# Two transformer blocks on one core: modulation rows spread in program order, the context split off the end of a feed-forward, and the query products put last

## The chip, the cores and the metric

The kernel runs on one core of a Trainium2 chip. The metric is the device time of one launch, in microseconds. Of the kernel before, three runs gave 2831.24, 2831.26 and 2832.66 us; the median is 2831.26 us.

## The reference

The program is a hybrid layer followed by a conditioned block, on 512 tokens of width 1024, all in fp32.

The first block normalizes 16 meta tokens and the 512 tokens, projects them, runs retention, differential attention and a short convolution side by side, merges the three by gates, and ends with a feed-forward `x + relu(norm(x) @ w_up)^2 @ w_down` of width 4096 and a norm.

The second block takes that result as its latent tokens, and 256 context tokens beside them. Nine modulation vectors of width 1024 steer it:

```python
m  = split(silu(c)     @ w_ada + b_ada, 9)     # for the latent tokens
mc = split(silu(c_ctx) @ w_ada + b_ada, 9)     # for the context
x     = residual(x,     swiglu(modnorm(x,     g[0], m[0],  m[1]),  w1, w3, w2), g[1], m[2],  0.5)
h_ctx = residual(h_ctx, swiglu(modnorm(h_ctx, g[0], mc[0], mc[1]), w1, w3, w2), g[1], mc[2], 0.5)
q, k, v, gates = project(modnorm(x, g[2], m[3], m[4]), modnorm(h_ctx, g[2], mc[3], mc[4]))
```

The feed-forward is 2816 wide. Then follow neighbourhood attention and attention from low-rank query and key latents (768 and 256 wide), a gated merge and a second feed-forward, for the latent tokens only. All of `m` is needed, and the first five vectors of `mc`.

## The kernel before

Activations lie with the model width on the 128 partitions in 8 slabs and the tokens along the free axis. Each fp32 operand is split into a high and a low part, and each product is three matmuls (high x high, high x low, low x high). Weights come as units of 512 KB by DMA from the SP queue into `raw`, three buffers deep; ScalarE writes the high part `whi` (line 132), VectorE or GpSimd the low part `wlo` (line 136). `low_parts(V, G)` lets the two take turns, `low_parts(V, V)` gives all to VectorE. Results collect in PSUM, in four buffers that take turns (`DEEP`), and are read out ("evacuated") by VectorE and ScalarE.

The class `Emitter` writes the program out. Its items are products (`gemm`), calls and background work. It keeps a program clock: each matmul adds its columns / 2.4 + 3 ns (`tick`). A background generator is advanced by one step each time that the clock has gained its pace (`background(fn, pace)`); `drain` writes out all that is left of it; `after(ns, fn)` delays a piece of work by that much of the program clock. What is written out in this order is then ordered on each engine by the framework's scheduler, which goes by program order but lets an instruction that it takes to be ready go ahead of others on its engine.

The stages that matter here, in order:

- **The feed-forward of the first block** (`up_evac`, `down_evac`, from line 1084): four groups g of 8 up and 8 down units, each unit 24 matmuls of 512 columns. An up result takes two VectorE steps (`ut`, lines 1045 and 1046), the high part by ScalarE (`uh`) and the low part (`ul`).
- **The modulation rows** (`ada_bg`, line 975): the product with `w_ada` isn't done on TensorE. Its 72 row tiles of 128 x 1024 (`wa`, 512 KB each, three buffers, loaded by SP) are multiplied with the spread conditioning `sb` and summed by one VectorE instruction (line 995). Tiles 0 to 39 are taken twice, for the context (`wx`) and the latents. That makes 112 such instructions and the coefficients `cf` after them. All run in the background of groups 0 to 2 of the first feed-forward, one in 2250 ns of the program clock, and are drained before group 3.
- **Block 2's first feed-forward** (`ffn`, `XC`): 22 hidden tiles in three groups (6, 8, 8). For each, `pair` makes two units (`w1`, `w3`) over 258 context columns and 512 latent columns; two of the columns carry the shift. Then `products` multiplies the hidden tiles with `w2`.
- **Its end** (`f1_tail`): the products of the last group come as context and second half of the latents (512 columns), then the first half (256). Beside the latter runs `update` (line 1174) for the 512 columns that are ready: norm, residual, and the next modulated input, in 11 slots of VectorE, ScalarE and GpSimd work.
- **Projections** (`kv`, line 1388, and after): key and value latents over context and second half, beside the `update` of the first half; drain; key and value latents over the first half, with the same weights loaded again; six query units; then key, value, rotated-query and query products, whose results are written to DRAM for the attention.

Of the kernel before, what the change touches and what calls it, by code (L numbers as in the profile page):

```python
# [14 lines left out]
D = 1024  # L15
# [243 lines left out]
def emit(tc, d, out, dbg=None, stop=None):  # L259
# [10 lines left out]
    def act(o, i, f=AF.Copy, **kw):  # L270
        A.activation(o, i, f, **kw)
# [684 lines left out]
    def mod(k, s=0):  # L956
        return S["modc"][:, s, 8 * k:8 * k + 8]

    def open_f():
        for n in ("m2", "bina", "xhl"):  # L960
            pools.close(n)
        p = S["hlx"] = pools.open("hlx")
        S["XH"] = p.tile([128, KT, 514], F32R, name="XH")
        S["XL"] = p.tile([128, KT, 514], F32R, name="XL")
        S["modc"] = p.tile([128, 2, 72], F32, name="modc")
        S["cf"] = p.tile([128, 9, 8], F32, name="cf")
        S["R4"] = p.tile([128, 768], F32, name="R4")
# [3 lines left out]
        S["CL"] = p.tile([128, KT, 258], F32R, name="CL")  # L971
        S["up"] = pools.open("up")
        S["ad"] = pools.open("ad")

    def ada_bg():

        p = S["ad"]
        sb = p.tile([128, 2, D], F32, name="sb")
        SP.dma_start(sb, d["cc"].partition_broadcast(128))
        act(sb, sb, AF.Silu)  # L980
        W, todo = [], list(range(72))

        def load():
            if todo:
                w = p.tile([128, D], F32, name="wa", tag="wa", bufs=3)
                SP.dma_start(w, d["wa"][todo.pop(0)])
                W.append(w)
        for _ in range(3):
            load()
        yield  # L990
        for j in range(72):
            w = W.pop(0)
            for s_ in ((1, 0) if j < 40 else (0,)):
                o = w if s_ == 0 else p.tile([128, D], F32, name="wx", tag="wx")
                V.tensor_tensor_reduce(o, w, sb[:, s_, :], 1.0, 0.0, ALU.mult, ALU.add,  # L995
                                       S["modc"][:, s_, j:j + 1])
                if s_ == 0:
                    load()
                yield
        V.tensor_add(S["modc"][:, 0, :], S["modc"][:, 0, :], col("bada", 0, 72))  # L1000
        V.tensor_add(S["modc"][:, 1, 0:40], S["modc"][:, 1, 0:40], col("bada", 0, 40))

        def gcol(i):
            return col("g", 8 * i, 8)
        for o, i, m_, s_ in ((AF0, 0, 1, 0), (A0C, 0, 1, 1), (A2X, 2, 4, 0), (A2C, 2, 4, 1), (A4, 4, 7, 0)):
            V.tensor_scalar_add(cf(o), mod(m_, s_), 1.0)
            V.tensor_mul(cf(o), cf(o), gcol(i))
        V.tensor_mul(cf(AF0), cf(AF0), col("final", 0, 8))
        for o, i, m_, s_, w in ((B1X, 1, 2, 0, 0.5), (B1C, 1, 2, 1, 0.5), (B3, 3, 5, 0, None), (B5, 5, 8, 0, 0.5)):
            V.tensor_mul(cf(o), mod(m_, s_), gcol(i))  # L1010
            if w is not None:
                V.tensor_scalar_mul(cf(o), cf(o), w)
        yield

    def shift_cols(kx, kc):
        todo = [(S["XH"], S["XL"], 512 + i, mod(kx)) for i in range(2)]
        if kc is not None:
            todo += [(S["CH"], S["CL"], 0, mod(kx)), (S["CH"], S["CL"], 1, mod(kc, 1))]
        for h_, l_, o, m_ in todo:
            act(h_[:, :, o], m_)  # L1020
            sub_lo(V, l_[:, :, o], m_, h_[:, :, o])

    def ctx_ops():

        pools.close("ad")
        p = S["fp"]
# [57 lines left out]
    em.call(open_f)  # L1084
    em.background(ada_bg, 2250)
    for g in range(4):
# [32 lines left out]
    def ffn(tag, w1, w3, w2, mode, ntok, pool, Rk, down, head, tail):  # L1119
# [26 lines left out]
        for gi, (k0, nk) in enumerate(grp):  # L1146
# [27 lines left out]
    def update(c0, c1, p, b, a, bc=None, ac=None, spilled=False, late=1500):  # L1174


        xe = min(c1, 512)
        n = xe - c0
        Ry, acc = S["Ry"][:, c0:c1], S["accy"][:, c0:c1]
# [8 lines left out]
        def parts(k):  # L1188

            yield S["y"][:, k, c0:xe], S["x"][:, k, c0:xe], b, a, S["XH"][:, k, c0:xe], S["XL"][:, k, c0:xe], 0  # L1190
            if ctx:
                yield S["y"][:, k, xe:c1], CR[k], bc, ac, S["CH"][:, k, 2:258], S["CL"][:, k, 2:258], n

# [71 lines left out]

    MQ = 96.0 ** -0.5

    def open_pj():
# [8 lines left out]
        p = S["pj"] = pools.open("pj", side="right")  # L1277
        S["QH"] = p.tile([128, 6, 512], F32R, name="QH")
        S["QL"] = p.tile([128, 6, 512], F32R, name="QL")
        S["Rq"] = p.tile([128, 512], F32, name="Rq")  # L1280
        S["aq"] = p.tile([128, 512], F32, name="aq")
        S["tmpq"] = p.tile([128, 512], F32, name="tmpq")
        for n_, w in (("rotT", 128), ("ropeC", 512), ("ropeS", 512)):
# [3 lines left out]
    def open_kvp():  # L1287
        pools.close("hid")
        p = S["kvp"] = pools.open("kvp")
        S["KH"] = p.tile([128, 2, 768], F32R, name="KH")  # L1290
# [5 lines left out]
        S["krt"] = p.tile([32, 768], F32, name="krt")  # L1296
        S["krs"] = p.tile([32, 2, 768], F32R, name="krs")

    def lat_evac(j, hi, lo, acc, g, nt, last, done):
# [118 lines left out]
    def open_na():  # L1418
        em.flush_after()
        pools.close("pj")  # L1420
        pools.close("kvp")
        p = S["onap"] = pools.open("onap", side="right")
# [425 lines left out]

    def f2_tail(products):
        products([(256, 256)])  # L1850
# [125 lines left out]
```

## Time and profile before

| | us |
|---|---|
| median of three runs | 2831.26 |
| profiled execution | 2835.28 |
| its span, first to last instruction | 2833.3 |

The profile is of one execution. Its own time is 2835.28 us, 2.0 us more than the span; the steps are summed against that. PE is TensorE, PEld its weight load, DVE VectorE, ACT ScalarE, POOL GpSimd, and SP the engine whose queue issues the DMAs. PEclk is the granted clock of TensorE as a share of 2.4 GHz. A wait in the trace is put down to what released it.

### The profile page before, as it was taken

Reading aid. Unit: us, or ns where it says so; the run is one execution under the profiler, and the core shown is the slowest. Engines: PE = TensorE matmul, PEld = TensorE weight load, DVE = VectorE, ACT = ScalarE, POOL = GpSimd, SP = SyncE. Lnnn points to the kernel's source line nnn. Section 1 sums busy time; section 2 is a strip of 40 time slices with the busy share of each in tenths; the row PEclk is TensorE's granted clock in tenths of the full one; section 3 lists DMA queues with packets and bytes.
Section 4 is the critical chain, followed back from the end, with each engine's and each line's share of the span. In section 5 each row is a group of like instructions: output and inputs, shape, how many; then the busy total and the mean of one; then the engine's idle time right before and its main releaser. Section 6 shows DMA issues by size and latency. Waiting matters only on the chain.

```text
span 2833.3 us, 42915 instructions
## 1 busy us (share of the span) xinstructions
PE 2736.0 (97%) x16308; PEld 2405.3 (85%) x16308; DVE 1620.0 (57%) x3318; ACT 1092.5 (39%) x2201; POOL 849.9 (30%) x710
## 2 busy tenths in 40 slices
PE   9999999999999889899999999979999999899997
PEld 8889988888878667788888888868889998899897
DVE  6554422377757999555223233496576876834346
ACT  4333322445534222243222122354455665633233
POOL 0223323433324233242111112442333224323224
PEclk9999999999999999999999999989999999999998
DMA  4222222443225658332121221334643424332324
GB/s 136 73 68 91 96 97 93 129 125 102 83 93 191 205 195 295 114 108 68 53 75 60 61 66 60 93 117 156 179 102 103 133 62 162 133 97 90 93 94 127
DMA packets 115998, 316.95 MB, mean 112 GB/s; under 512 B 21680, under 2 KB 35376, under 8 KB 115536
## 3 DMA queue, kind: packets, MB, share of 16 engines
q1 hardware_dynamic: 115792, 314.21, 35.5%
q8 instruction: 129, 2.11, 0.3%
q14 instruction: 77, 0.63, 0.1%
HBM read 279.09 MB, written 13.83 MB: 103 GB/s over the span
## 4 chain that ended last, share of the span: by engine, by line
PE 80%; DVE 14%; issue 3%; ACT 2%; DMA 0%; POOL 0%; POOLq 0%; DVEq 0%; SPq 0%; ACTq 0%
PE psg L231 49%; PE pss L231 22%; DVE wlo L136 2%; DVE wa L995 2%; DVE wx L995 1%; PE pss L277 1%; PE pst L827 1%; PE pss L278 1%; PE pss L279 1%; PE pst L1731 1%; PE pst L1717 1%; PE pss L1528 1%; PE pst L824 0%; DVE ut L1045 0%; DVE mg L1224 0%
## 5 line engine op out<-in xcount | busy, mean ns | idle before, releaser
L136 POOL TENSOR_TENSOR wlo<-raw,whi 128x512 fp32r<-128x512 f32 (+1 forms) x442 | 580.1, 1313 | 1568.4 <-ACT whi L132 1527.4
L132 ACT ACTIVATE whi<-raw 128x512 fp32r<-128x512 f32 (+1 forms) x844 | 522.7, 622 | 927.8 <-PE psg L231 588.8
L136 DVE TENSOR_TENSOR wlo<-raw,whi 128x512 fp32r<-128x512 f32 (+1 forms) x402 | 314.0, 782 | 452.6 <-ACT whi L132 451.9
L231 PE MATMUL psg<-xl,whi 128*128 128x264 f32 (+2 forms) x1104 | 362.7, 329 | 0.9 <-DVE xl L403 0.9
L231 PE MATMUL psg<-xh,whi 128*128 128x264 f32 (+2 forms) x1104 | 361.4, 328 | 1.7 <-ACT whi L132 1.2
L231 PE MATMUL psg<-xh,wlo 128*128 128x264 f32 (+2 forms) x1104 | 361.7, 328 | 0.0
L231 PE MATMUL psg<-XH,whi 128*128 128x256 f32 (+3 forms) x984 | 308.2, 313 | 1.8 <-DVE ft L1136 1.0
L231 PE MATMUL psg<-XH,wlo 128*128 128x256 f32 (+3 forms) x984 | 308.2, 313 | 0.0
L231 PE MATMUL psg<-XL,whi 128*128 128x256 f32 (+3 forms) x984 | 307.8, 313 | 0.0
L231 PEld LDWEIGHTS psg<-xh,whi 128*128 128x128 f32 x1104 | 209.0, 189 | 18.8 <-ACT whi L132 1.4
L231 PEld LDWEIGHTS psg<-xl,whi 128*128 128x128 f32 x1104 | 209.1, 189 | 18.5 <-DVE xl L403 1.5
L231 PEld LDWEIGHTS psg<-xh,wlo 128*128 128x128 f32 x1104 | 209.2, 190 | 17.0 <-DVE wlo L136 0.2
L231 PE MATMUL pss<-XL,whi 128*128 128x256 f32 (+2 forms) x600 | 191.3, 320 | 6.1 <-DVE XL L1208 6.1
L231 PEld LDWEIGHTS psg<-XH,whi 128*128 128x128 f32 (+1 forms) x984 | 185.4, 188 | 11.5 <-issue 2.4
L231 PEld LDWEIGHTS psg<-XH,wlo 128*128 128x128 f32 (+1 forms) x984 | 185.8, 189 | 10.5 <-issue 0.2
L231 PEld LDWEIGHTS psg<-XL,whi 128*128 128x128 f32 (+1 forms) x984 | 185.8, 189 | 9.3
L231 PE MATMUL pss<-XH,wlo 128*128 128x256 f32 (+2 forms) x600 | 191.4, 319 | 1.2 <-DVE wlo L136 1.2
L231 PE MATMUL pss<-XH,whi 128*128 128x256 f32 (+2 forms) x600 | 190.9, 319 | 0.5 <-DVE fs L1128 0.5
L231 PEld LDWEIGHTS pss<-XL,whi 128*128 128x128 f32 x600 | 114.9, 192 | 14.3 <-DVE XL L1208 7.3
L231 PEld LDWEIGHTS pss<-XH,wlo 128*128 128x128 f32 x600 | 115.4, 192 | 10.1 <-DVE wlo L136 1.6
L231 PEld LDWEIGHTS pss<-XH,whi 128*128 128x128 f32 x600 | 114.9, 192 | 7.5 <-DVE fs L1128 0.7
L231 PE MATMUL pss<-hh,wlo 128*128 128x256 f32 (+1 forms) x296 | 101.8, 344 | 7.5 <-DVE wlo L136 7.5
(558 smaller groups left out, 6444.6 us busy)
## 6 DMA issues: line engine op xcount, KB each, us to landing
raw<-w SPq DMA_DIRECT2D x142, 512.0 KB, 3.3
raw<-wi SPq DMA_DIRECT2D x96, 512.0 KB, 3.3
wa<-wa SPq DMA_DIRECT2D x72, 512.0 KB, 4.2
raw<-wq SPq DMA_DIRECT2D x38, 512.0 KB, 3.5
raw<-wu SPq DMA_DIRECT2D x32, 512.0 KB, 4.2
raw<-wd SPq DMA_DIRECT2D x32, 512.0 KB, 4.1
raw<-wb SPq DMA_DIRECT2D x24, 512.0 KB, 3.2
raw<-wo SPq DMA_DIRECT2D x24, 512.0 KB, 4.0
```

The source lines that it names most:

```text
L132: s.nc.scalar.activation(h, raw, AF.Copy)
L136: eng.tensor_sub(l, raw, h.bitcast(F32))
L231: nc.tensor.matmul(out, l, r, start=(k == 0 and m == 0), stop=(k == it.kt - 1 and m == 2))
L277: T.matmul(o, wh, xh, start=first, stop=False)
L278: T.matmul(o, wh, xl, start=False, stop=False)
L279: T.matmul(o, wl, xh, start=False, stop=last)
L827: T.matmul(o, x[:, c, :], vs[:, c, :], start=False, stop=c == b and m == 1)
L995: V.tensor_tensor_reduce(o, w, sb[:, s_, :], 1.0, 0.0, ALU.mult, ALU.add, S["modc"][:, s_, j:j + 1])
L1528: T.matmul(ps[:, a:a + cw], q, k[:, c0:c0 + cw], start=m == 0, stop=m == 1)
L1717: T.transpose(ps[:, 128 * c:128 * c + 128], P_[:, 128 * (c0 + c):128 * (c0 + c) + 128], ident)
L1731: T.matmul(o[:, 0:256], v[:, c, :], x[:, c, :], start=c == 0 and m == 0, stop=c == 5 and m == 1)
```

## The change

The modulation rows are made in two parts. Tiles 0 to 15 (32 instructions, `m[0]` and `m[1]`) stay in the first feed-forward, at a pace of 8000 ns; tiles 16 to 71 (80 instructions) go beside block 2's first feed-forward, at 4800 ns. Each row instruction is tied behind the VectorE instruction that was written out before it. The row tiles have two buffers instead of three.

In block 2's first feed-forward the third group makes the pairs of the latents alone, then the latent products, then the pairs and products of the context, with the `w1` and `w3` units loaded again. Beside the context runs the `update` of all 512 latent columns, at a pace of 2600 ns. Then come the six query units, with the `update` of the context beside them, then the drain, the key and value latents in one pass, the rotated-query products, the key and value products, and the query products. The query latents' tiles get a pool of their own.

```diff
-    def ada_bg():
+    def ada_bg(j0, j1):
...
-        W, todo = [], list(range(72))
+        W, todo = [], list(range(j0, j1))
...
-                w = p.tile([128, D], F32, name="wa", tag="wa", bufs=3)
+                w = p.tile([128, D], F32, name="wa", tag="wa", bufs=2)
...
-                V.tensor_tensor_reduce(o, w, sb[:, s_, :], 1.0, 0.0, ALU.mult, ALU.add,
-                                       S["modc"][:, s_, j:j + 1])
+                tc.keep_in_program_order(
+                    V.tensor_tensor_reduce(o, w, S["sb"][:, s_, :], 1.0, 0.0, ALU.mult, ALU.add,
+                                           S["modc"][:, s_, j:j + 1]))
...
-    em.background(ada_bg, 2250)
+    em.background(lambda: ada_bg(0, 16), 8000)
...
-            for j in range(head(pair) if gi == 0 else 0, nk):
-                pair(j, mode)
+            if gi < 2 or ntok == 512:
+                for j in range(head(pair) if gi == 0 else 0, nk):
+                    pair(j, mode)
             if gi == 2:
-                tail(products)
+                tail(products, pair)
...
-    def f1_tail(products):
-        products([(256, 512)])
+    def f1_tail(products, pair):
+        for j in range(8):
+            pair(j, XO, "x")
+        em.drain()
+        products([(0, 512)])
         em.low_parts(V, V)
-        em.call(lambda: shift_cols(3, 3))
-        em.background(lambda: update(256, 768, S["fpa"], B1X, A2X, B1C, A2C, True), 1150)
-        products([(0, 256)])
+        em.call(lambda: shift_cols(3, None))
+        em.background(lambda: update(0, 512, S["fpa"], B1X, A2X, spilled=True), 2600)
+        for j in range(8):
+            pair(j, XC[0:1], "c")
+        products([(512, 256)])
         em.drain()
 
     em.call(open_f1)
+    em.background(lambda: ada_bg(16, 72), 4800)
...
     em.call(open_kvp)
-    em.depth(DEEP, 2)
-    em.background(lambda: update(0, 256, S["fpa"], B1X, A2X, spilled=True), 1200)
-    kv(XC_A)
-    em.depth(DEEP, 2)
+    em.low_parts(V, G)
+    em.call(lambda: shift_cols(3, 3, False))
+    em.background(lambda: update(512, 768, S["fpa"], None, None, B1C, A2C), 1200)
+    for j in range(6):
+        proj(d["wq"][12 + j], 128, XO, lat_evac(j, "QH", "QL", "aq", "gq", 512, j == 5, rq_done), "cq")
     em.drain()
     em.call(lambda: dumps((("x2", lambda: S["x"]),)))
     em.call(open_pj)
-    em.low_parts(V, G)
-    kv(X_B)
-    em.depth(DEEP)
-    for j in range(6):
-        proj(d["wq"][12 + j], 128, XO, lat_evac(j, "QH", "QL", "aq", "gq", 512, j == 5, rq_done), "cq")
+    kv(XC)
+    for j in range(2):
+        em.gemm(d["wuq"][4 + j], 128, lambda si: (S["QH"], S["QL"]), FULL, qr_evac(j), kt=6)
...
-    for j in range(2):
-        em.gemm(d["wuq"][4 + j], 128, lambda si: (S["QH"], S["QL"]), FULL, qr_evac(j), kt=6)
```

## Rows read from the trace of the kernel before

**Rows 1.** Page, part 1: busy time, share of the span, instructions of each engine.

```profile
PE 2736.0 (97%) x16308; PEld 2405.3 (85%) x16308; DVE 1620.0 (57%) x3318; ACT 1092.5 (39%) x2201; POOL 849.9 (30%) x710
```

**Rows 2.** Busy time by stretch; columns as in the first line.

```profile
core 0: us, PE busy (x) PEld busy (x) DVE busy (x) ACT busy (x) POOL busy (x), PEclk, DMA share, GB/s
884.03:985.85 101.82, 93.86 (x396) 74.42 (x394) 98.56 (x145) 30.76 (x50) 34.33 (x22) 0.95 0.64 211
985.85:1092.30 106.45, 94.29 (x385) 73.92 (x384) 103.92 (x153) 25.21 (x44) 33.36 (x20) 0.94 0.67 226
1092.30:1194.38 102.08, 91.99 (x390) 73.72 (x388) 72.71 (x111) 28.32 (x56) 34.88 (x25) 0.95 0.57 191
1194.38:1283.83 89.45, 89.16 (x388) 72.47 (x388) 49.77 (x64) 37.81 (x64) 44.76 (x32) 1.00 0.33 103
1283.83:1642.56 358.73, 358.73 (x2037) 312.40 (x2036) 121.39 (x215) 97.00 (x169) 62.85 (x58) 1.00 0.20 62
1642.56:1777.54 134.98, 134.98 (x769) 118.06 (x768) 49.78 (x88) 38.21 (x65) 26.64 (x24) 1.00 0.20 63
1777.54:1822.35 44.81, 44.81 (x194) 36.04 (x193) 13.32 (x18) 15.07 (x24) 17.86 (x14) 1.00 0.33 95
1822.35:1923.33 100.98, 80.73 (x556) 73.58 (x554) 88.66 (x205) 51.76 (x119) 40.58 (x36) 0.90 0.34 107
1923.33:1996.20 72.87, 70.46 (x400) 60.67 (x399) 48.32 (x100) 33.61 (x69) 18.92 (x21) 0.98 0.57 188
...
884.03:1194.38 310.35, 280.14 (x1168) 222.06 (x1166) 275.19 (x407) 84.29 (x150) 102.56 (x67) 0.95 0.63 209
```

**Rows 3.** Waits of TensorE, 884 to 1194 us: total us, times, longest.

```profile
PE psg L231 <- ACT uh L271: 18.2, 5, 5.1
```

**Rows 4.** The chain that ended last, in order of time: start, us, what.

```profile
805.80 11.20 PE pss L231 x48
...
1293.58 1.80 PE pst L349 x4
...
1304.74 8.43 PE psg L231 x48
...
1926.56 5.75 PE pss L231 x48
```

**Rows 5.** Groups of VectorE instructions, 884 to 1194 us: count | busy us, mean ns.

```profile
L995 DVE CUSTOM_DVE_ANT_0 wa<-wa,sb 128x1024 f32<-128x1024 f32 x72 | 104.8, 1460 | 2.6 <-DMA wa<-wa 2.0
L995 DVE CUSTOM_DVE_ANT_0 wx<-wa,sb 128x1024 f32<-128x1024 f32 x40 | 58.8, 1471 | 0.0
...
L995 DVE DVE_READ_ACCUMULATOR2_ANT modc<- 128x1 f32 x112 | 8.8, 78 | 0.0
```

**Rows 6.** The tile wa: idle time of its engine until the landing; landing time.

```profile
  DMA wa<-wa: 2.0, 4
...
DMA to landing us min/median/max: 3.1/4.2/7.6
```

**Rows 7.** Waits of the SP queue, whole span.

```profile
SPq L105 <- POOL wlo L136: 1102.5, 354, 11.7
```

**Rows 8.** Groups of VectorE instructions, 1822 to 1900 us.

```profile
L1224 DVE SCALAR_TENSOR_TENSOR mg<-y,cf,mg 128x256 f32<-128x256 f32 x16 | 15.7, 989 | 1.8 <-POOL y L1227 1.8
L136 DVE TENSOR_TENSOR wlo<-raw,whi 128x512 fp32r<-128x512 f32 x20 | 15.5, 774 | 0.7 <-ACT whi L132 0.5
L1208 DVE SCALAR_TENSOR_TENSOR XL<-mg,cf,XH 128x256 fp32r<-128x256 f32 x16 | 10.9, 685 | 0.0
```

**Rows 9.** Groups of VectorE instructions, 1296 to 1390 us.

```profile
L1137 DVE SCALAR_TENSOR_TENSOR fs<-ft,bt,fs 128x512 f32<-128x512 f32 x6 | 9.1, 1525 | 0.2
...
L1137 DVE SCALAR_TENSOR_TENSOR fs<-ft,bt,fs 128x256 f32<-128x256 f32 x6 | 2.9, 483 | 0.2
L1136 DVE TENSOR_TENSOR ft<-pss,R 128x256 f32<-128x256 f32 x6 | 2.5, 415 | 0.0
...
L1113 DVE COPY bt<-pss 128x2 f32<-128x2 f32 x6 | 0.9, 157 | 10.5 <-PE pss L231 10.5
```

More of the change, by code (lines that the diff above doesn't have):

```diff
@@ L971, in open_f @@
         S["CL"] = p.tile([128, KT, 258], F32R, name="CL")
+        S["ad"] = pools.open("ad")
         S["up"] = pools.open("up")
-        S["ad"] = pools.open("ad")
-    def ada_bg():
+    def ada_bg(j0, j1):
         p = S["ad"]
-        sb = p.tile([128, 2, D], F32, name="sb")
-        SP.dma_start(sb, d["cc"].partition_broadcast(128))
-        act(sb, sb, AF.Silu)
-        W, todo = [], list(range(72))
+        if j0 == 0:
+            S["sb"] = p.tile([128, 2, D], F32, name="sb")
+            SP.dma_start(S["sb"], d["cc"].partition_broadcast(128))
+            act(S["sb"], S["sb"], AF.Silu)
+        W, todo = [], list(range(j0, j1))
         def load():
             if todo:
-                w = p.tile([128, D], F32, name="wa", tag="wa", bufs=3)
+                w = p.tile([128, D], F32, name="wa", tag="wa", bufs=2)
                 SP.dma_start(w, d["wa"][todo.pop(0)])
                 W.append(w)
-        for _ in range(3):
-            load()
+        load()
+        load()
         yield
-        for j in range(72):
+        for j in range(j0, j1):
             w = W.pop(0)
@@ L999, in ada_bg @@
                 yield
-        V.tensor_add(S["modc"][:, 0, :], S["modc"][:, 0, :], col("bada", 0, 72))
-        V.tensor_add(S["modc"][:, 1, 0:40], S["modc"][:, 1, 0:40], col("bada", 0, 40))
+        for s_, j2 in ((0, j1), (1, min(j1, 40))):
+            V.tensor_add(S["modc"][:, s_, j0:j2], S["modc"][:, s_, j0:j2], col("bada", j0, j2 - j0))
         def gcol(i):
@@ L1005, in ada_bg, with shift_cols @@
         for o, i, m_, s_ in ((AF0, 0, 1, 0), (A0C, 0, 1, 1), (A2X, 2, 4, 0), (A2C, 2, 4, 1), (A4, 4, 7, 0)):
-            V.tensor_scalar_add(cf(o), mod(m_, s_), 1.0)
-            V.tensor_mul(cf(o), cf(o), gcol(i))
-        V.tensor_mul(cf(AF0), cf(AF0), col("final", 0, 8))
+            if j0 <= 8 * m_ < j1:
+                V.tensor_scalar_add(cf(o), mod(m_, s_), 1.0)
+                V.tensor_mul(cf(o), cf(o), gcol(i))
+                if o == AF0:
+                    V.tensor_mul(cf(o), cf(o), col("final", 0, 8))
         for o, i, m_, s_, w in ((B1X, 1, 2, 0, 0.5), (B1C, 1, 2, 1, 0.5), (B3, 3, 5, 0, None), (B5, 5, 8, 0, 0.5)):
-            V.tensor_mul(cf(o), mod(m_, s_), gcol(i))
-            if w is not None:
-                V.tensor_scalar_mul(cf(o), cf(o), w)
+            if j0 <= 8 * m_ < j1:
+                V.tensor_mul(cf(o), mod(m_, s_), gcol(i))
+                if w is not None:
+                    V.tensor_scalar_mul(cf(o), cf(o), w)
         yield
-    def shift_cols(kx, kc):
-        todo = [(S["XH"], S["XL"], 512 + i, mod(kx)) for i in range(2)]
+    def shift_cols(kx, kc, lat=True):
+        todo = [(S["XH"], S["XL"], 512 + i, mod(kx)) for i in range(2)] if lat else []
         if kc is not None:
@@ L1023, in ctx_ops @@
     def ctx_ops():
-        pools.close("ad")
         p = S["fp"]
@@ L1177, in update @@
         xe = min(c1, 512)
-        n = xe - c0
+        n = max(xe - c0, 0)
         Ry, acc = S["Ry"][:, c0:c1], S["accy"][:, c0:c1]
@@ L1188, in parts @@
         def parts(k):
-            yield S["y"][:, k, c0:xe], S["x"][:, k, c0:xe], b, a, S["XH"][:, k, c0:xe], S["XL"][:, k, c0:xe], 0
+            if n:
+                yield S["y"][:, k, c0:xe], S["x"][:, k, c0:xe], b, a, S["XH"][:, k, c0:xe], S["XL"][:, k, c0:xe], 0
             if ctx:
-                yield S["y"][:, k, xe:c1], CR[k], bc, ac, S["CH"][:, k, 2:258], S["CL"][:, k, 2:258], n
+                yield S["y"][:, k, 512:c1], CR[k], bc, ac, S["CH"][:, k, 2:258], S["CL"][:, k, 2:258], n
         load(0)
@@ L1277, in open_pj @@
         p = S["pj"] = pools.open("pj", side="right")
[L1278 to L1282, printed above, removed]
         for n_, w in (("rotT", 128), ("ropeC", 512), ("ropeS", 512)):
@@ L1288, in open_kvp @@
         pools.close("hid")
+        pools.close("ad")
         p = S["kvp"] = pools.open("kvp")
@@ L1297, in open_kvp @@
         S["krs"] = p.tile([32, 2, 768], F32R, name="krs")
+        p = S["pjq"] = pools.open("pjq")
+        S["QH"] = p.tile([128, 6, 512], F32R, name="QH")
+        S["QL"] = p.tile([128, 6, 512], F32R, name="QL")
+        S["Rq"] = p.tile([128, 512], F32, name="Rq")
+        S["aq"] = p.tile([128, 512], F32, name="aq")
+        S["tmpq"] = p.tile([128, 512], F32, name="tmpq")
     def lat_evac(j, hi, lo, acc, g, nt, last, done):
@@ L1420, in open_na @@
         pools.close("pj")
+        pools.close("pjq")
         pools.close("kvp")
@@ L1847, in finish, with f2_tail @@
             yield
-    def f2_tail(products):
+    def f2_tail(products, pair):
         products([(256, 256)])
```

## Prediction

> **What bounds the kernel now.** I read the page's engine shares first. TensorE is busy 97% of the span and VectorE 57% [rows 1], so only two things can move the time: matmul work added or removed, and the stretches where TensorE waits or runs at a lower clock. Next I cut the span by stage at the matmuls' operands [rows 2]. The first block's feed-forward has four groups of equal matmul work. Three, with the modulation rows beside them, took 101.82, 106.45 and 102.08 us at a clock of 0.94 to 0.95; the fourth, without, took 89.45 us at 1.00. In the three, VectorE is busy 275.19 of 310.35 us, 89%; in the fourth, 49.77 of 89.45. Block 2's first feed-forward (1283.83 to 1822.35) shows no loss: TensorE busy throughout, clock 1.00, VectorE near a third. Then 1822.35 to 1923.33 loses again: TensorE 80.73 of 100.98 us, clock 0.90, VectorE 88.66. The waits of TensorE in the first lossy stretch name the tail of the result chain (uh, written by ScalarE after two VectorE steps): five waits, 18.2 us [rows 3]. The reader is to see that VectorE, 57% busy overall, is the bound in two stretches, and that the stretch between them has room on it.
>
> The chain of waits gives matmul prices at full clock: 48 matmuls of 512 columns in 11.20 us, so 233.3 ns each; 24 of 258 with 24 of 512 in 8.43; 48 of 256 and 258 in 5.75, so 119.8 ns each [rows 4].
>
> **1. Modulation rows thinned in the first block's feed-forward.** A row instruction took 1.46 us (x72) and 1.47 (x40), with an accumulator read of 0.08 [rows 5]: 1.54 us, 172 us for 112. Thirty-two stay, 49 us, at one per 8 us of program time instead of 2.25. VectorE's load falls to (275 - 172 + 49) in 271 us, 56%, just what the fourth group has with no loss. So the three groups should take 3 x 89.45 = 268.4, plus about 1 us of matmuls of the norm that only the first group holds, plus 2 us for rows that fall into a result chain: 271.4, a gain of **39.0 us**. Bounds on that 2: nothing, and the loss per row of today, 42.0 / 112 = 0.375 us, which gives 12. I take a value near the lower end, because the loss comes from a full queue, and the fourth group is the nearest row to the new load.
>
> **2. Eighty rows move to block 2's first feed-forward.** They are 123 us of VectorE. From 1283.83 on, the two groups, the latent half of the third and the latent products will last 358.7 + 92.0 + 44.8 = 495.5 us. VectorE does at most 121.39 + 49.78 + 13.32 = 184.5 us there today [rows 2], so 308 of 495 us after, 62%. What lies behind a row is a result of a matmul or a low part; four result buffers turn over in about two units, 16.9 us, against 1.5 for a row. The cover ends only where products need the last hidden tile at once, three times: I take **+2 us**; bounds 0 and 80 x 0.375 = 30. Each row's weights go through SP, 512 KB each, and SP's queue stands behind weight loads that wait for their buffer: 354 waits for GpSimd's low parts, 1102.5 us, so 3.1 each [rows 7]. With two buffers a row's load has two slots, 9.6 us of program time (about 10.4 real: 24 of 258 and 24 of 512 columns count 7.84 and take 8.43); a landing took 4.2 us median [rows 6]. So 3.1 + 4.2 fits.
>
> **3. The third group split.** Sixteen units of 8.43 (134.98) become 16 of 5.75 (92.0) and 16 of 24 x 0.1198 = 2.87 (46.0): +3.0 us of TensorE, and sixteen 512 KB loads and 32 pairs of splits more. Products stay 44.8 + 23.0.
>
> **4. From the third group to the last query product.** Today 134.98 + 44.81 + 100.98 + 72.87 = 353.6 us. TensorE's own work after: 92.0 + 44.8 + 46.0 + 23.0; six query units 6 x 5.75 = 34.5; keys and values once, 3 x 8.43 = 25.3 (twice before, by halves); the products from the query and key latents, six units of 18 at 233.3 ns, 25.2, four of 6 at 119.8 and 6 at 233.3, 8.5, and 36 at 233.3, 8.4. Sum 307.7. Norm and rotation matmuls put in between: some ten at about 1 us (two 512-column spreads took 1.80 [rows 4]), 10. The reordering of the last four costs and saves nothing: the same matmuls, and the query's norm is long done when they begin.
>
> The stall is the open term. VectorE's work beside the context pairs, by rows of the lossy stretch [rows 8] and of the feed-forward [rows 9]: 32 low parts at 0.774 = 24.8; eight pairs of two multiplies (0.415) and one fused step (0.483) = 10.5; the update of 512 columns, eight fused steps at 1.525 (the 512-wide row) and eight at 2 x 0.685 = 23.2; three more at 0.774 = 2.3; some 46 short ones at 0.157 = 7.2. Together 68.0 us beside 46.0 of TensorE. Context products: 16 x 0.774 + 8 x 0.415 = 15.7 beside 23.0. Query units with the context's update: twelve results at 0.415 + 0.415 + 0.685, 18.2; six low parts, 4.6; 8 x (0.989 + 0.685) = 13.4; some 34 short ones and four of 0.415, 7.0; together 43.2 beside 34.5. Sum 126.9 of VectorE, and as much idle as in today's lossy stretch, 12.3, makes 139.2; TensorE needs 103.5 and 4.5 of inserts: 31 us late. The last query results and their norm, about 6 us, may trail under the key products that follow, which are light on VectorE: 25. Later waits as in 1923.33 to 1996.20 (72.87 less 23.0, 42.1 and 5): 3. So 307.7 + 10 + 25 + 3 = 345.7, a gain of **8 us**. Bounds for the 25: 5, with the 483 ns of today's quiet rows in place of 989 for steps beside GpSimd, and 45, if the idle share of today's stretch (12%) is doubled by the longer chain. So the tail ends between -28 and +12.
>
> One rule bears on that term. Fused steps of 256 columns took 483 ns in the quiet feed-forward and 989 beside the update's GpSimd work [rows 8, 9], while those with one input in PSUM stayed at 415. The Trainium skill, "SBUF — State Buffer", section "Who interferes with whom", says that VectorE's instructions with two SBUF inputs and GpSimd's reads exclude each other for a whole instruction, whichever begins first; the trace agrees. By that rule, an estimate: 56 such instructions of the context pairs, each meeting GpSimd (40.58 busy of 100.98 us [rows 2]) and waiting about half of one, come to 4 us more than my sum.
>
> **Sum**, against the profiled execution: 2835.28 - 39.0 + 2 - 8 = 2790.3. That execution was 4.0 us above the median of 2831.26, so on the scale of the median: **2786 us**.
>
> **Rivals.** *A, the context pairs cost more.* VectorE holds TensorE through pairs, products and query units for 45 us: the tail is +12, the sum 2835.28 - 39 + 2 + 12 - 4 = 2806. For it: 68 us of VectorE beside 46 of TensorE, and today's stretch lost a fifth. Against: the same update today stands beside 23 us of products, so it gets more room. *B, a row costs what it costs today wherever it stands.* 12 and 30 us: 2786 + 10 + 28 = 2824. That is also the case in which the rows don't spread. For it: a row is 1.2 to 2.3 us at the head of an in-order queue. Against: today they run into a queue that is 89% full, and the fourth group shows none of it. *C, slower: a tied row waits for its weights at the head of VectorE's queue.* Today an early row is only picked when the scheduler thinks it ready; in the trace 72 rows waited 2.0 us in all [rows 6]. Two buffers instead of three, a place in SP's queue behind waiting loads, and nothing behind the row may run. VectorE has 495 - 308 = 187 us to spare, 3.3 us per load for 56; the forecast's gain of 45 is used up at (187 + 47) / 56 = 4.2 us per load, and from there the kernel is slower. At 5 us: 280 - 187 = 93 over, 2786 - 2 + 93 = 2877. Against: slots of 10.4 us for landings of 3.1 to 7.6.
>
> **How the numbers follow.** Forecast 0.68, A 0.17, B 0.06, C 0.05, and 0.04 that the tail or the clock gives more than I count, below 2762. The forecast's own range, 2762 to 2804, is the first step between 0 and 12, the second between 0 and 10, the tail between -28 and +4, not all at one end. The range down to 2762 and up to 2814 takes in A and half of the way to B. About 0.2% (5.7 us) is what can be told from no change. Faster: forecast, A, the 0.04 and half of B, 0.92; same: the other half, 0.03; slower: C, 0.05.
>
> **What would show it.** The three groups near 90 us each at clock 1.00, with VectorE under 65%; a row every 8 us of the program there and every 4.8 in block 2's feed-forward; that feed-forward's units still 8.43 us, and VectorE's waits for wa under 1 us each. The context pairs lasting 60 to 75 us where 46 would do, TensorE waiting for low parts of VectorE, and the clock below 1 there. Wrong, if uh still holds TensorE in the first block, if units of the second feed-forward stretch, or if the pairs run at 2.87 us each.

## The result, and the profile after

The changed kernel takes 2802.85 us (median of four runs, 2799.99 to 2805.63), against 2831.96 us for the kernel before in the same comparison (2831.24 to 2833.31): a ratio of 0.9897, 95% interval 0.9879 to 0.9914. It is 29 us faster. The forecast was 2786 us.

The profiled execution of the kernel after took 2805.63 us, 2.8 us above that median; its stretches are set against those of [rows 2]. They come from one execution each, so a difference of a microsecond in one stretch says little.

The page of the kernel after, part 1, columns as in [rows 1]:

```profile
PE 2727.6 (97%) x16620; PEld 2413.6 (86%) x16620; DVE 1621.5 (58%) x3363; ACT 1107.1 (39%) x2224; POOL 853.1 (30%) x717
```

The shares have hardly moved: VectorE did as much work as before, elsewhere. Busy time by stretch of the kernel after, columns in the first line:

```profile
core 0: us, PE busy (x) PEld busy (x) DVE busy (x) ACT busy (x) POOL busy (x), PEclk, DMA share, GB/s
884.75:975.30 90.55, 90.46 (x395) 73.28 (x394) 56.54 (x78) 31.04 (x50) 27.66 (x22) 1.00 0.42 138
975.30:1063.67 88.37, 88.37 (x385) 72.08 (x384) 54.26 (x64) 24.41 (x40) 26.30 (x20) 1.00 0.38 125
1063.67:1152.05 88.38, 88.38 (x386) 72.08 (x384) 55.58 (x66) 24.41 (x40) 26.06 (x20) 1.00 0.40 125
1152.05:1247.91 95.86, 91.43 (x391) 73.90 (x390) 56.91 (x87) 43.49 (x81) 49.09 (x37) 0.98 0.37 114
1247.91:1606.67 358.76, 358.76 (x2038) 312.41 (x2037) 210.05 (x354) 96.16 (x169) 68.22 (x58) 1.00 0.39 125
1606.67:1698.73 92.06, 92.06 (x770) 92.06 (x768) 58.55 (x124) 33.43 (x65) 31.62 (x24) 1.00 0.49 155
1698.73:1743.53 44.80, 44.80 (x195) 36.05 (x193) 12.43 (x19) 14.95 (x24) 18.06 (x14) 1.00 0.30 95
1743.53:1802.73 59.20, 50.62 (x396) 47.95 (x394) 54.11 (x97) 34.38 (x64) 24.93 (x19) 1.00 0.51 161
1802.73:1830.99 28.26, 25.76 (x204) 24.52 (x203) 21.07 (x49) 15.63 (x32) 6.31 (x8) 1.00 0.54 168
1830.99:1877.70 46.71, 39.24 (x302) 38.52 (x301) 40.38 (x94) 23.46 (x55) 23.41 (x25) 0.93 0.27 86
1877.70:1911.51 33.81, 31.90 (x172) 23.76 (x171) 18.36 (x58) 10.73 (x23) 3.86 (x3) 0.95 0.07 20
1911.51:1965.75 54.24, 48.66 (x200) 37.01 (x198) 32.61 (x53) 20.59 (x38) 10.60 (x9) 0.94 0.73 238
```

The first four lines are the groups of the first block's feed-forward, the fifth the first two groups of block 2's, then the latent pairs, the latent products, the context pairs, the context products, the six query units, the key and value latents, and the last products. The ledger, before to after: first three groups 310.35 to 267.30 (a gain of 43.05); fourth group 89.45 to 95.86 (6.4 lost); the two groups with the 80 rows 358.73 to 358.76; from the third group to the last query product 353.64 to 359.08 (5.4 lost); the start and the rest of the span 1.7 lost. That is 29.5 of the 29.65 us between the two profiled executions.

In the first three groups no wait of TensorE is left, where uh alone held it for 18.2 us [rows 3]. The fourth group has two waits that were not there before; waits of TensorE in the kernel after, 1150 to 1205 us (total us, times, longest):

```profile
PE pst L330 <- POOL acc L921: 3.6, 1, 3.6
PE pst L349 <- DVE sq L340: 0.9, 1, 0.9
```

Line 330 is the four one-column matmuls that sum the squares of the context for its norm (`ctx_ops`). They stand in TensorE's queue between the units, and nothing behind them ran until GpSimd had added the last square. Two things had moved. TensorE came to the sums at 1165.4 us (1168.96 less the wait), where it had come at 1194.0 before; and GpSimd was done at 1168.9, where it had been done at 1158.6 before. The second follows the rows. The last two of the 32 that stay give the last of the context's coefficients; they were still to come when the group began at 1152.05, the last ended at 1156.4, and GpSimd's last addition came 12.5 us behind it. Before, the last of the 112 rows ended at 1145.6, 49 us ahead of the fourth group, and the last addition came 13.0 us behind it. Either shift alone would have left no wait (an estimate from these times: 6.8 us to spare with GpSimd as before, 25 with TensorE as before). The last row, GpSimd's last additions and the sums, before (start, us):

```profile
1143.28 2.28 DVE L995 CUSTOM_DVE_ANT_0 wa<-wa,sb 128x1024 f32<-128x1024 f32 x1
1156.80 1.75 POOL L921 TENSOR_TENSOR acc<-acc,sq 128x256 f32<-128x256 f32 x2
1194.02 0.50 PE L330 MATMUL pst<-ones,acc 128*128 128x1 f32 x4
```

The same row and additions, after:

```profile
1155.20 1.22 DVE L998 CUSTOM_DVE_ANT_0 wa<-wa,sb 128x1024 f32<-128x1024 f32 x1
1167.32 1.59 POOL L921 TENSOR_TENSOR acc<-acc,sq 128x256 f32<-128x256 f32 x2 [0.77 <-ACT sq L271]
```

TensorE's timeline there, after (in brackets the idle time before):

```profile
1168.96 0.60 PE L330 MATMUL pst<-ones,acc 128*128 128x1 f32 x4 [3.57 <-POOL acc L921]
...
1169.98 0.39 PE L231 MATMUL pss<-zh,whi 128*128 128x512 f32 x1
1170.21 0.40 PE L231 MATMUL pss<-zl,whi 128*128 128x512 f32 x1
...
1172.41 0.63 PE L231 MATMUL pss<-zl,whi 128*128 128x512 f32 x1
1172.84 0.63 PE L231 MATMUL pss<-zh,wlo 128*128 128x512 f32 x1
```

Read the starts: 0.23 us apart at first, then, from 1170.71 to 1174.09, 0.43 apart, half the rate, and then 0.23 again; the granted clock over that stretch is 0.51. So the wait costs 3.6 us and then some 1.5 more: eight matmuls at 1.2 instead of 2.4 GHz.

The rows themselves; the tile wa in the kernel after:

```profile
L998 DVE CUSTOM_DVE_ANT_0 wa<-wa,sb x72: 1212/1218/2301, 913.2 to 1670.6; 128x1024 f32<-128x1024 f32 x72
L998 DVE CUSTOM_DVE_ANT_0 wx<-wa,sb x40: 1210/1218/2300, 905.8 to 1500.6; 128x1024 f32<-128x1024 f32 x40
...
  DMA wa<-wa: 0.7, 1
...
DMA to landing us min/median/max: 3.1/3.5/5.4
```

They run over 765 us instead of 251, and VectorE waited for weights once, 0.7 us ([rows 6]: 2.0).

### The profile page after: what moved, and what is told of

Its sections match the earlier page's. It is cut to its first block, busy times and chain, and to the rows that moved or that the text cites. A ratio compares the mean times of both kernels' runs of the same rounds, so it can differ in the third digit from the quotient of the medians.

```text
span 2803.8 us, 43694 instructions
## 1 busy us (share of the span) xinstructions
PE 2727.6 (97%) x16620; PEld 2413.6 (86%) x16620; DVE 1621.5 (58%) x3363; ACT 1107.1 (39%) x2224; POOL 853.1 (30%) x717
## 4 chain that ended last, share of the span: by engine, by line
PE 86%; DVE 8%; issue 2%; ACT 2%; DMA 1%; POOL 0%; SPq 0%; POOLq 0%; DVEq 0%; ACTq 0%
PE psg L231 51%; PE pss L231 26%; DVE wlo L136 1%; PE pss L277 1%; PE pst L827 1%; PE pss L278 1%; PE pss L279 1%; PE pst L1745 1%; PE pst L1731 1%; PE pss L1542 1%; ACT whi L132 1%; PE pst L824 0%; PE pst L349 0%; PE pst L330 0%; DVE XL L1216 0%
## 5 line engine op out<-in xcount | busy, mean ns | idle before, releaser
L132 ACT ACTIVATE whi<-raw 128x512 fp32r<-128x512 f32 (+1 forms) x871 | 541.1, 622 | 925.3 <-PE psg L231 566.5
L231 PE MATMUL psg<-XL,whi 128*128 128x256 f32 (+2 forms) x1040 | 320.1, 308 | 3.3 <-DVE XL L1216 3.3
L231 PE MATMUL psg<-XH,whi 128*128 128x256 f32 (+2 forms) x1040 | 319.1, 307 | 1.5 <-DVE ft L1142 1.0
L231 PE MATMUL psg<-XH,wlo 128*128 128x256 f32 (+2 forms) x1040 | 319.7, 307 | 0.3 <-DVE wlo L136 0.3
L231 PEld LDWEIGHTS psg<-xh,whi 128*128 128x128 f32 x1104 | 209.0, 189 | 18.6 <-ACT whi L132 1.2
L231 PEld LDWEIGHTS psg<-XL,whi 128*128 128x128 f32 x1040 | 197.5, 190 | 12.1 <-DVE XL L1216 4.0
L231 PEld LDWEIGHTS psg<-XH,wlo 128*128 128x128 f32 x1040 | 197.4, 190 | 9.9 <-issue 1.2
L231 PEld LDWEIGHTS psg<-XH,whi 128*128 128x128 f32 x1040 | 197.0, 189 | 10.0 <-issue 2.3
L231 PEld LDWEIGHTS pss<-XL,whi 128*128 128x128 f32 x648 | 122.4, 189 | 4.8
L231 PEld LDWEIGHTS pss<-XH,whi 128*128 128x128 f32 x648 | 122.1, 188 | 4.7
L271 ACT ACTIVATE hh<-fs 128x256 fp32r<-128x256 f32 x96 | 43.1, 449 | 161.7 <-DVE fs L1143 161.7
```

The costliest lines, as they stand in the source:

```text
L132: s.nc.scalar.activation(h, raw, AF.Copy)
L231: nc.tensor.matmul(out, l, r, start=(k == 0 and m == 0), stop=(k == it.kt - 1 and m == 2))
```

## The experiments

Each run was timed beside the kernel before on the same chip; ratios are to that. The median of the kernel before was 2832.67 us in the comparison of the first four, 2832.8 for the next four, 2834.04 for e9 to e11 and 2834.11 for e12.

**The two parts alone.** Kernel e1_rows_only has the rows as after and the end of block 2's first feed-forward, projections included, as before. Kernel e2_tail_only is the reverse.

```diff
# e1 (shortened): before, with the tie, the two buffers and
-    em.background(ada_bg, 2250)
+    em.background(lambda: ada_bg(0, 16), 8000)
+    em.background(lambda: ada_bg(16, 72), 4800)
# e2 (shortened): after, with the rows untied, three buffers and
-    em.background(lambda: ada_bg(0, 16), 8000)
-    em.background(lambda: ada_bg(16, 72), 4800)
+    em.background(ada_bg, 2250)
```

> Rows split in two and tied, as in the change; the end of block 2's first feed-forward and the projections as before. Theory (the gain is the rows alone, the new tail costs a little): the three groups near 88.5 us each, the fourth near 96, the second feed-forward unchanged, the tail near the 353.6 us of before: about 2832 - 43 + 6 + 1 = 2796 us, some 6 below the whole change. Rival (the new tail gains about 8 us, as forecast, and rows beside the second feed-forward cost it that): 2808 to 2812.

> All 112 rows at the old place and pace, untied, with three buffers; the new tail. Theory: the tail alone is +5 us, 2837 (2834 to 2841). Rival (the tail gains by itself): 2824. If the two parts don't add up to the whole change within 4 us, they meet somewhere.

Measured: e1 2799.12 us, 0.9879 [0.9865, 0.9894], 33.5 us faster than before; e2 2841.70 us, 1.0029 [1.0019, 1.0039], 9.0 slower. The rows are the whole gain. That the new end of the feed-forward costs time is shown by e2; the intervals of e1 and of the kernel after overlap. Its stretch (third group to the last query product, with the two groups ahead of it, since the third is split) takes 712.37 us before, 714.19 in e1, 716.89 in e2 and 717.84 after: 3.6 us of loss with the rows moved, 4.5 without. In e2 the first block's three groups are 3.0 us longer as well, and the stages behind the last query product 3.7. Those stages take 840.1 to 840.9 us in six of the eight profiles with the new end (838.1 in the kernel after, 837.1 in e11 below), and 836.8 to 837.3 in all six with the old one.

**The context's norm.** Kernel e3_norm_late is the kernel after, with the sums written out 26 us of the program clock later; e8_rows_norm is e1 with the same edit.

```diff
-        rnorm(S["R4"][:, 512:768], S["acc"][:, 0:256], D, tmp, gap=2800)
+        em.after(26000, lambda: rnorm(S["R4"][:, 512:768], S["acc"][:, 0:256], D, tmp, gap=2800))
```

> The changed kernel with the context's norm in the first feed-forward's fourth group written out 26 us of program time later, so that its sums come behind 119 more matmuls on TensorE; all else the same. Theory (the fourth group lost 6.4 us because TensorE stood 3.6 us before the norm's sums, waiting for GpSimd's last addition, and then ran at half clock): the group falls from 95.9 to 89 to 90 us and the time by 6, to 2797. Rival (the last rows, drained at the start of the group, hold VectorE): the group stays at 95 to 96, the time at 2803.

> Rows split and tied, the old tail, and the context's first norm 26 us later: e1_rows_only and e3_norm_late together. Theory (independent): 2799.1 - 3.4 = 2795.7. Rival (the earlier stage only shifts the old tail's waits): 2799.

Measured: e3 2799.45 us, 0.9879 [0.9864, 0.9894]; e8 2790.72 us, 0.9853 [0.9835, 0.9870]. The intervals with and without the edit overlap, so the whole times alone don't show it; the stretch does. The fourth group of e3, columns as above, and all of TensorE's waits in its first half:

```profile
1147.24:1238.81 91.57, 89.59 (x392) 72.83 (x390) 57.16 (x87) 43.29 (x81) 50.09 (x37) 1.00 0.39 120
```

```profile
PE pst L349 <- DVE sq L340: 2.0, 1, 2.0
```

95.86 has become 91.57, at clock 1.00: the wait for the sums is gone and with it the slow stretch behind it; a wait of 2.0 us for the spread of the norm is what is left over the 89.45 of before. The rival, that the group stays at 95 to 96, fell. In e1 the same group took 97.38, in e8 91.58; e8 came out 5 us below its theory.

**Tie or pace.** The change thins the rows by two means: a slower pace in the writing-out, and the tie to VectorE's order. Kernel e4_no_pin is the kernel after without the tie; e5_tie_only is the kernel before (2250 ns, three buffers, all rows in the first block) with it.

```diff
# e4: after, with
-                tc.keep_in_program_order(
-                    V.tensor_tensor_reduce(o, w, S["sb"][:, s_, :], 1.0, 0.0, ALU.mult, ALU.add,
-                                           S["modc"][:, s_, j:j + 1]))
+                V.tensor_tensor_reduce(o, w, S["sb"][:, s_, :], 1.0, 0.0, ALU.mult, ALU.add,
+                                       S["modc"][:, s_, j:j + 1])
```

> The changed kernel without the tie of a row behind the VectorE instruction written out before it; both paces as in the change. Theory (the pace spreads the rows, the tie only moves each by an instruction or two): within 5 us of the changed kernel, 2798 to 2808, rows still spread. Rival (without the tie the rows run ahead and gather): the three groups slower than 90 us each, 2810 or more.

> The kernel before with the tie alone: all 112 rows in the first feed-forward at 2250 ns, three buffers. Untied rows were seen to run up to 500 us ahead of where they are written out, so the tie, and not the pace, spreads them. Theory (the three groups lose to VectorE's load, 89%, and the tie leaves the load): 2825 to 2838, the groups still 100 us or more. Rival (they lose because a row slips between the two steps of a result; the tie ends that): the groups near 93, the time 2805 to 2815.

Measured: e4 2843.08 us, 1.0030 [1.0020, 1.0041]; e5 2825.59 us, 0.9971 [0.9959, 0.9983]. My theory for e4, that the pace does the spreading, fell. The tile wa in e4:

```profile
L997 DVE CUSTOM_DVE_ANT_0 wa<-wa,sb x72: 1206/1224/2318, 891.6 to 1174.7; 128x1024 f32<-128x1024 f32 x72
...
  DMA wa<-wa: 18.8, 20
```

All 112 rows ran in the first block, though 80 of them were written out behind it; block 2's first feed-forward began at 1283.66. The scheduler takes an instruction whose operands it thinks ready ahead of others, and a row needs only its weights and the conditioning. Without the tie the kernel takes what e2 takes, which has all rows there by the program: split and pace alone bring nothing. In e5 the rows are in order but as many as before. Its four groups:

```profile
881.61:983.53 101.92, 95.35 (x395) 75.54 (x394) 92.30 (x130) 30.74 (x50) 32.61 (x22) 0.95 0.58 195
983.53:1081.62 98.09, 92.38 (x386) 73.80 (x384) 89.64 (x118) 23.96 (x40) 31.30 (x20) 0.97 0.57 185
1081.62:1182.06 100.44, 92.51 (x390) 73.56 (x388) 91.49 (x135) 29.48 (x55) 39.63 (x25) 0.95 0.75 255
1182.06:1276.31 94.25, 90.51 (x389) 73.47 (x389) 54.34 (x88) 38.45 (x69) 44.84 (x32) 0.98 0.35 112
```

The first three take 300.45 us, against 310.35 before [rows 2] and 267.30 after, with VectorE 91% busy. So the lighter load is worth most of the gain, 33 us, and the tie alone 10, of which the fourth group gives 4.8 back (94.25 for 89.45). The whole time says the same: e5 is 7 us faster than before, clear of noise. Whether those 10 us come from the order or from rows spread more evenly (VectorE's work in the third group is 91.49 us for 72.71) was not separated. The fourth group's loss has a wait of its own, at the spread of the context's norm: its steps on VectorE stood among the last rows, which ended at 1188.9 us, 6.9 behind the start of the group:

```profile
PE pst L349 <- ACT sq L271: 3.7, 1, 3.7
```

Here TensorE came to the group 33 us later behind the start of the first than it did after, and the group still lost. In e4 and e2, where untied rows run ahead, it took 89.40 and 89.45.

**The low parts beside the context pairs.** Kernel e6_low_vg is the kernel after, with the low parts of the context's weights taken by VectorE and GpSimd in turn, instead of by VectorE alone.

```diff
         products([(0, 512)])
-        em.low_parts(V, V)
```

> The changed kernel with the low parts beside the context pairs and products by turns on VectorE and GpSimd, not all on VectorE. Theory (VectorE's load is what stretches the pairs, 54 us busy in 59.2): 24 low parts less on VectorE, about 18 us; the pairs fall from 59.2 to 50 to 54 and the products from 28.3 to 25, the time by 5 to 10, to 2793 to 2798. Rival (GpSimd's extra 24 x 1.3 = 31 us hold the update's chain and block VectorE's two-input steps): no gain or a loss, 2800 to 2812.

Measured: 2812.82 us, 0.9927 [0.9912, 0.9943], about 10 slower than after: the rival's loss, 0.8 above its range. The context pairs and their main wait:

```profile
1741.99:1808.39 66.40, 53.98 (x396) 51.63 (x394) 58.47 (x87) 34.66 (x65) 49.66 (x35) 0.92 0.48 147
```

```profile
PE pss L231 <- POOL wlo L136: 6.8, 2, 5.6
```

Fourteen of the 29 low parts left VectorE, and it was busy 58.47 us instead of 54.11: a low part took 1099 ns instead of 830, the update's 512-column steps 1434 and 1287 instead of 1176 and 981.

**GpSimd out of the update.** Kernel e11_update_v goes the other way: the twelve instructions of the latents' update that GpSimd did go to VectorE. Kernel e12_old_v does the same to the old update of e9 (below).

```diff
# e11 (e12: "or ctx" instead of "or c0 == 0")
-                (V if k == KT - 1 else G).tensor_add(acc, acc, SQ.pop(k))
+                (V if k == KT - 1 or c0 == 0 else G).tensor_add(acc, acc, SQ.pop(k))
-                (V if slot % 4 == 3 else G).tensor_mul(y, y, Ry)
+                (V if slot % 4 == 3 or c0 == 0 else G).tensor_mul(y, y, Ry)
```

> The changed kernel, but in the update of the 512 latent columns (beside the context pairs) the twelve instructions that GpSimd did (six multiplies of y, six sums of squares) go to VectorE. GpSimd is then nearly idle there. Theory (GpSimd's work is what makes VectorE's instructions with two SBUF operands long): the fused 256-column step falls from 920 ns to near 483, the low part from 830 towards 770, the update's steps from 1176 to under 1100; against about 9 us of added work VectorE saves 5 to 6, is busy 57 to 58 of some 61 us, and the kernel takes 2803 to 2807 us. Rival (GpSimd is not the cause): prices stay, VectorE 63 us busy, the context pairs 68 us or more, the kernel 2811 to 2815 us.

Measured: 2800.02 us, 0.9883 [0.9868, 0.9897], against 0.9897 [0.9879, 0.9914] for the kernel after. The whole times don't separate the two; the groups of VectorE do. Context pairs of the kernel after, count | busy us, mean ns:

```profile
L136 DVE TENSOR_TENSOR wlo<-raw,whi 128x512 fp32r<-128x512 f32 x29 | 24.0, 830 | 2.3 <-ACT whi L132 1.0 <-PE pss L231 1.0
L1232 DVE SCALAR_TENSOR_TENSOR mg<-y,cf,mg 128x512 f32<-128x512 f32 x8 | 9.4, 1176 | 0.8 <-POOL y L1235 0.8
...
L1143 DVE SCALAR_TENSOR_TENSOR fs<-ft,bt,fs 128x256 f32<-128x256 f32 x7 | 6.4, 920 | 0.0
L1142 DVE TENSOR_TENSOR ft<-psg,R 128x256 f32<-128x256 f32 x4 | 1.6, 412 | 0.0
```

The same of e11, and its window:

```profile
L136 DVE TENSOR_TENSOR wlo<-raw,whi 128x512 fp32r<-128x512 f32 x29 | 20.1, 695 | 2.1 <-ACT whi L132 1.0 <-PE pss L231 1.0
L1232 DVE SCALAR_TENSOR_TENSOR mg<-y,cf,mg 128x512 f32<-128x512 f32 x8 | 7.4, 920 | 0.0
...
L1143 DVE SCALAR_TENSOR_TENSOR fs<-ft,bt,fs 128x256 f32<-128x256 f32 x6 | 2.9, 476 | 0.0
L1142 DVE TENSOR_TENSOR ft<-psg,R 128x256 f32<-128x256 f32 x4 | 1.6, 412 | 0.0
```

```profile
1742.47:1796.99 54.52, 50.84 (x397) 48.02 (x396) 50.37 (x108) 36.14 (x66) 10.26 (x7) 1.00 0.55 175
```

With more work VectorE is busy 50.37 us instead of 54.11. The fused step of 256 columns is back at 476 ns, the 483 of the quiet feed-forward [rows 9]; the step with an input in PSUM is 412 in both. That is what the Trainium skill, "SBUF — State Buffer", section "Who interferes with whom", says: VectorE's instructions with two SBUF inputs and GpSimd's reads exclude each other. Here moving twelve instructions onto the engine that bounds the stretch, at 0.68 us each, made it less busy, and the stretch shorter by 4.7 us.

**The waits that are left.** Kernel e7_waits is e3 with four buffers for the value tiles and the sums of the context's second norm (the update beside the query units) written out later. Kernel e9_best is e8 with the four buffers. Kernel e10_rot_back is the kernel after, with the two rotated-query products back behind the value products.

```diff
# e7, e9
-        o = p.tile([128, 8, 2, 64], F32R, name="vst", tag="vst", bufs=2)
+        o = p.tile([128, 8, 2, 64], F32R, name="vst", tag="vst", bufs=4)
# e7: late=1500 is the default
-    em.background(lambda: update(512, 768, S["fpa"], None, None, B1C, A2C), 1200)
+    em.background(lambda: update(512, 768, S["fpa"], None, None, B1C, A2C, late=8000), 1200)
```

```diff
# e10: the first two lines move behind the value products
-    for j in range(2):
-        em.gemm(d["wuq"][4 + j], 128, lambda si: (S["QH"], S["QL"]), FULL, qr_evac(j), kt=6)
...
     em.gemm_tok(d["wuv"], 512, lambda si: (S["KH"], S["KL"]), [(128 * c, 128) for c in range(6)], v_evac, kt=2)
+    for j in range(2):
+        em.gemm(d["wuq"][4 + j], 128, lambda si: (S["QH"], S["QL"]), FULL, qr_evac(j), kt=6)
```

> The changed kernel with the context's first norm written out 26 us later (as in e3_norm_late), the norm after the context's update written out 8 us after it instead of 1.5, and four buffers instead of two for the value results. Theory (TensorE stands 6.3 us before that second norm's sums and 3.8 us for a value buffer, and its clock halves behind both): the six query units fall from 46.7 to about 40, the last products from 54.2 to about 48; with the 3.4 us of e3_norm_late, 2803 - 3.4 - 12 = 2788. Rival (VectorE is behind by that much anyway, the wait moves to the next user): 2797 to 2800.

> The changed kernel with one edit undone: the two rotated-query products stand behind the key and value products again, not in front of them. The prediction held that this order costs and saves nothing: 2802.9 us within 3. Rival: in front, they are TensorE work that is light on VectorE while the key latents' norm is made, so with them behind the key products wait for that norm, at a lower clock behind it: 4 to 8 us slower, 2807 to 2811 us, the loss between the query units and the query products.

TensorE's waits in the kernel after, 1832 to 1966 us, and in e7, 1826 to 1956:

```profile
PE pst L330 <- DVE accy L1218: 6.3, 1, 6.3
PE pss L231 <- DVE vst L1401: 3.8, 1, 3.8
...
```

```profile
PE pst L349 <- DVE RF L340: 5.2, 1, 5.2
...
```

Busy time in the kernel after, beside the first of these waits and behind it, columns as above:

```profile
1856.00:1863.00 7.00, 1.15 (x5) 1.15 (x6) 6.96 (x15) 3.47 (x9) 4.10 (x4) 0.79 0.36 122
1863.00:1868.00 5.00, 5.00 (x28) 5.00 (x28) 4.83 (x14) 2.15 (x5) 2.70 (x3) 0.61 0.29 80
```

Measured: e7 2795.77 us, 0.9866 [0.9851, 0.9882], between theory and rival and nearer to the rival. The value wait goes and stays away, and the last products fall from 54.24 to 47.24 us (48 in the theory). The norm wait does not go: put off, it comes back at the next matmul of the same norm, 5.2 us for 6.3, and the query units take 46.5 us as before (40 in the theory). In those 7 us of the kernel after VectorE is busy 6.96: it is behind, and the later place in TensorE's queue did not mend that. e10 took 2805.48 us, 0.9898 [0.9882, 0.9915]: the order of these products costs and saves nothing, as predicted.

**The best version.**

> The rows split and tied as in the changed kernel, the end of block 2's first feed-forward as before, the context's norm written out 26 us later, and four buffers for the value tiles. In the last of these kernels without the fourth buffer (2790.7 us) TensorE waited 2.3 us once for a value tile. Theory: that wait and the clock behind it go, about 3 us: 2788 us, groups and the rest unchanged. Rival: the value tiles are written out by a queue that is the bound, the wait only moves: 2790 to 2792 us.

> The best kernel so far (rows split and tied, old end of the feed-forward, context's norm later, four value buffers; 2787.6 us) with the update of context and second half, beside the last latent products, done without GpSimd: its six multiplies and six sums of squares of 512 columns go to VectorE. In the changed kernel the same move gave VectorE shorter instructions (fused 256-column step 920 to 476 ns, low part 830 to 695) and the stretch 6 us. Theory: the same prices hold here: 24 low parts x 0.07 + 16 x 0.4 + 16 x 0.1 = 9.7 us saved against 12 x 0.68 = 8.2 us added, and the chain through GpSimd is shorter; the stretch of 124.2 us loses 2 to 6 us, kernel 2782 to 2786 us. Rival: VectorE is already 83% busy there and the multiplies stand at the head of its queue, in front of the low parts: 0 to 5 us slower, 2788 to 2793 us.

Measured: e9 2787.61 us, 0.9835 [0.9820, 0.9849]; e12 2784.03 us, 0.9823 [0.9810, 0.9837]. Both beat the kernel after; between the two the whole times don't decide. In e9 the value wait of e8 is gone, but the intervals of e8 and e9 overlap, so what it was worth is not shown. The stretch that e12 edits, in e9 and in e12:

```profile
1778.83:1903.00 124.17, 103.98 (x747) 96.84 (x746) 103.54 (x238) 63.11 (x145) 51.75 (x47) 0.92 0.31 96
```

```profile
1778.23:1899.23 121.00, 107.35 (x747) 99.49 (x746) 99.10 (x250) 63.01 (x145) 34.91 (x35) 0.89 0.31 98
```

With twelve instructions more VectorE is busy 4.4 us less, and the stretch is 3.2 us shorter; TensorE's granted clock is lower, 0.89 for 0.92, and why was not tried. Both keep the rows of the change and the old end of the feed-forward; they are 46 and 50 us below the kernel before.

## Why the prediction was right and wrong

The direction and most of the mechanism held; the time came out 17 us above the forecast, close to rival A's 2806, but not for A's reason.

- **The three groups: right, 43.05 us for 39.0.** VectorE was 62% busy where 56% was predicted, and lost nothing. The residual of 2 us for rows in a result chain was nothing, and the second and third group took 88.4, a microsecond less than the fourth group of before, from which they were priced. What the step did not say is that the pace alone would have done nothing (e4): rival B named the case in which the rows don't spread and priced it at 2824; it measured 2843.
- **The eighty rows in block 2: right, 0.03 us for 2.** VectorE was busy 281.0 of 495.6 us up to the latent products, 57% (62% predicted), and the units took as long as before. With that B falls: rows cost time beside a VectorE that was 89 to 91% busy, and none beside one at 57 to 62%.
- **The tied rows' weights (rival C): fell**, one wait of 0.7 us.
- **The third group's split: right**, 92.06 and 44.80 for 92.0 and 44.8.
- **The fourth group: not in the sum at all, 6.4 us lost.** The prediction took it as unchanged because its own work is. But the change moved both ends of a wait in it: with [rows 3]'s waits gone, TensorE came 28.6 us earlier to the context's sums, and with the rows spread to the group's start and beyond, GpSimd had the last square 10.4 us later. The kernel before shows one wait in the group, of 0.3 us. Of the two steps that failed this is one (the later waits, below, are the other): I asked what is late next inside the three groups, and not behind them. That the wait is the loss is shown by e3 and e8; that late rows cost this group time even where TensorE is not early, by e5 (4.8 us, at another wait of the same norm). No run moved the end of the rows alone.
- **Context pairs, products and query units: right in sum, 134.2 us for 133.0** (103.5, 4.5 and 25). A, which held TensorE there for 20 us more, falls. That the sum came out is partly luck: VectorE's work was put at 126.9 us and measured 115.6, and the 18.6 us in which it was idle made up for that. The pairs took 59.20 us at clock 1.00, where 60 to 75 and a clock below 1 were foretold; TensorE did wait there for VectorE's low parts. By e7 the norm's wait of 6.3 us is VectorE being behind.
- **The later waits: mis-sized, about 15 us for 3.** Key and value latents and the last products took 88.05 us, where 25.3 + 42.1 + 5.5 of inserts + 3 = 76 were predicted. TensorE was idle for 7.5 of them (33.81 + 54.24 less 31.90 + 48.66); of the other 7.6 some 4.5 are its clock, 0.95 and 0.94 (an estimate: these shares of its busy time). The prediction priced these waits from the last stretch of the kernel before, in another order and behind another update. In e7, with two more buffers (and its other edits), the value wait is gone and the last 72 matmuls take 16.80 us, their full rate, for 19.62. Why that wait is 3.8 us here and 2.3 with the old end (e8) was not isolated.
- **So the tail: a forecast gain of 8, a loss of 5.4 in its own stretch**, inside the bounds (-28 to +12), with the wrong sign. The largest error of the prediction is there, and e2 shows it without the rows, 4.5 us: that half of the change should have been left out.
- **The rule on SBUF** was weighed as 4 us on top of the context's sum, without the steps from 56 instructions to 4 us; the sum was not exceeded, because it already used prices taken beside GpSimd. e11 shows that the rule was worth more as a way to a better kernel than as a term.

Against the profiled execution, the forecast of 2790.3 and the measured 2805.63 differ by 15.3: -4.1 in the three groups, +6.4 in the fourth, -2.0 in block 2, +13.4 in the tail, +1.7 at the start and behind.

Open: why the three groups are 3.0 us longer in e2 (1.7 in e4, which also has untied rows and the new tail), why the stages behind the last query product are some 3.5 us longer in most profiles with the new tail, and the lower clock in e12.

## What to carry to other kernels

Work that hangs on nothing but its weights isn't spread by where the program writes it out: look at its first and last start in the trace, and tie it if they are early. After a stall is taken away, walk on along the engine that was late to the next instruction that depends on another engine, and ask whether the other engine will be as early there as it was; work that was spread out may be what it waits for. And where VectorE bounds a stretch in which GpSimd also works in SBUF, moving work off VectorE can make it busier, and moving work onto it can free it.

## What the hardware showed that was not expected

- One wait of 3.6 us of TensorE was followed by eight matmuls of 512 columns at 0.43 us each instead of 0.23; after one of 6.3 us the granted clock was 0.61 over 5 us (1863 to 1868).
- The sum-product instruction of 128 x 1024 has a median of 1.218 us and a longest of 2.301 in the kernel after, and the means of [rows 5], 1460 and 1471, are a mix of the two. The trace shows what stood beside the long ones: all 24 above 1.3 us in the kernel after, and all 30 in the kernel before, began while a GpSimd instruction on SBUF was running, and ended 1.08 us behind its end; of the 88 short ones after none began so, and of the 82 before one, 0.08 us from the end. GpSimd's instruction and the row behind it, after (start, us):

```profile
936.83 1.29 POOL L136 TENSOR_TENSOR wlo<-raw,whi 128x512 fp32r<-128x512 f32 x1 [4.30 <-ACT whi L132]
```

```profile
936.91 2.29 DVE L998 CUSTOM_DVE_ANT_0 wx<-wa,sb 128x1024 f32<-128x1024 f32 x1
```

- In e11 the six low parts of hidden tiles left to GpSimd beside the context pairs took 1493 ns each instead of 940: the engine that lost instructions got slower in those that it kept. Why was not isolated.
